# SSD decay factors made during the gate products and carried through DRAM, and a new placement of the scan's first tiles

## The chip, the cores and the metric

One core of one Trainium2 chip runs the whole layer as one program. The metric is the device time of that program in microseconds (us), as the median over runs. Before the change it is 1986.23 us (three runs, 1985.98 to 1989.51).

## The reference, cut to what matters

The layer is a bidirectional hybrid block on 512 positions and 2048 channels in float32: a Mamba-2 SSD branch and a latent attention branch, merged by sigmoid gates. The change touches the diagonal blocks of the SSD scan. For a chunk of 128 positions and one head:

```
da    = dt * a
a_cs  = cumsum(da)                      # along the chunk
lmat  = exp(segsum(da))                 # lower triangle: exp of sums of da between s and l
cb    = einsum("bclgn,bcsgn->bcgls", cc, bc)
y_diag = einsum("bcgls,bgjcls,bcsgjp->bclgjp", cb, lmat, xd)
```

The scan runs forward and, on flipped sequences with its own `dt` and `a`, backward; both results are added. There are 32 heads in 4 groups and 4 chunks. The decay factors `lmat` depend only on `dt` and `a`, which are known long before the scan needs them.

## The kernel before

**Stages.** The program first normalizes `x` and makes `dt` (to about 110 us of the trace), then the three gate products `wz`, `wgs`, `wga` (to about 563 us), then the scan of the four groups, interleaved with projections that fill TensorE (to about 1120 us), then attention, two output projections and the last product. Float32 products are made of three fp32r matmuls: high by high, high by low, low by high.

**How a weight reaches TensorE.** A chunk of 128x1024 weights is loaded by SyncE's DMA queue (L493, tiles `X`, `Y` and `wraw`). ScalarE casts it to its high part `wh` (L457), VectorE subtracts to get the low part `wl` (L458), and TensorE runs 12 matmuls on it (L603 to L605). `wh` and `wl` have three buffers each. The gate products are Strassen products in column pairs: `pair` (from L689) makes seven products P1, P5, P6, P2, P3, P7, P4 of four chunks each, so 28 chunks, and there are three gates with two pairs each. Between products VectorE adds weight chunks (`X` plus `Y` L720, `X` plus `wraw` L724) and results (L650, L655, L678, L736, L757), and GpSimd's queue issues DMAs that add a second block onto a loaded chunk in place (`w_more`, L530) and pre-added weights for later products (L509, L510). Functions hung on `hooks` run after a product by name.

**How the scan makes its factors.** `ssd_group` (from L958) loops over chunks `c` and halves `q` of a group's eight heads. `da_load` broadcasts four heads' rows of `da` from DRAM to 128 partitions, once for each direction (`da0`, `da1`, L1089). `seg_make` runs one cumulative sum with a mask over each (`tensor_tensor_scan`, L1098), adds both (L1101), takes the exponential on ScalarE (L1102, tile `E`), and multiplies `E` into `G` (L1109), the weights of the matmuls `yb` (L1119). There are 32 such factors `E` of 128x512.

**What sets the order.** TensorE's order is written by hand. The other engines' orders come from a list scheduler: it takes operations by priority (program place, moved earlier by `high_priority`) as soon as its own model has their inputs and buffers ready, and the result is fixed in the program. On the chip each engine runs its list in order and waits at whatever is not ready. `keep_in_program_order` pins single instructions. The pool tag `st` (in `gp`) has three tiles of 128x512; before, it serves evictions and is nearly unused in the gate products. Pools are laid over memory of closed pools, and a new tile waits for the old tiles that it covers.

## Time and profile before

| | |
|---|---|
| median of three runs | 1986.23 us |
| the profiled execution, by its own time | 1987.53 us |
| its span in the profile | 1985.8 us |
| TensorE busy | 1933.5 us, 97% |
| VectorE busy | 1476.5 us, 74% |
| ScalarE busy | 1029.3 us, 52% |
| GpSimd busy | 246.3 us, 12% |

All positions below are us from the start of that span. A busy time is the union of an engine's instructions; TensorE's instructions overlap, so its busy share says little about how full it is, and the idle time in front of an instruction, with what ended it, says more. The line numbers are those of the kernel before.

### The profile page before, as it was taken

What the parts mean: (1) busy time and instruction counts of PE and PEld (TensorE: products, weight loads), DVE (VectorE), ACT (ScalarE), POOL (GpSimd) and SP (SyncE); (2) the same over time, 40 slices, a digit from 0 to 9 for tenths busy, and PEclk for the clock granted to TensorE, in tenths of its full rate; (3) what the DMA queues carried; (4) which work ended last, traced back from release to release, by engine and by line L of the source; (5) the groups of instructions that cost most, each with busy time, mean ns of one, the idle gap of its engine ahead of it and who ended that gap; (6) DMA issues with size and microseconds to landing.
All of it is one profiled execution on the core that took longest, in us unless ns stands there. A gap on an engine that the chain in (4) does not pass through costs nothing.

```text
span 1985.8 us, 24464 instructions
## 1 busy us (share of the span) xinstructions
PE 1933.5 (97%) x8834; PEld 1593.3 (80%) x8834; DVE 1476.5 (74%) x2064; ACT 1029.3 (52%) x1527; POOL 246.3 (12%) x309
## 2 busy tenths in 40 slices
PE   7999999999999999999999999999989999999997
PEld 5878888888878878877878878888877778888886
DVE  7876676676759879798785667676776889879467
ACT  6445445444464757747657344444455455444353
POOL 0011001001012020120210101111011111100011
PEclk9999999999999999999999999999999999999999
DMA  5569659569654635655554857787378787847446
GB/s 215 168 198 251 177 159 252 159 166 248 155 174 142 198 122 163 213 182 182 162 165 143 244 149 206 206 223 192 90 219 311 234 271 283 295 140 241 167 87 158
DMA packets 169545, 382.81 MB, mean 193 GB/s; under 512 B 16400, under 2 KB 66256, under 8 KB 169232
## 3 DMA queue, kind: packets, MB, share of 16 engines
q1 hardware_dynamic: 103680, 234.02, 35.2%
q0 software_dynamic: 30656, 103.30, 22.9%
q10 hardware_dynamic: 35088, 43.94, 6.2%
q8 instruction: 69, 1.13, 0.2%
q14 instruction: 52, 0.43, 0.1%
HBM read 329.22 MB, written 98.04 MB: 215 GB/s over the span
## 4 chain that ended last, share of the span: by engine, by line
PE 79%; DVE 9%; DMA 5%; issue 4%; ACT 2%; POOL 1%; SPq 0%; ACTq 0%; DVEq 0%; POOLq 0%
PE P L604 11%; PE P L605 11%; PE P L603 11%; PE xbc L167 4%; PE xbc L168 4%; PE xbc L169 4%; PE za L169 2%; PE za L167 2%; PE za L168 2%; DVE sum L1098 2%; PE qkv L167 1%; PE qkv L169 1%; PE f L1603 1%; PE f L1604 1%; PE qkv L168 1%
## 5 line engine op out<-in xcount | busy, mean ns | idle before, releaser
L457 ACT CAST wh<-X 128x1024 fp32r<-128x1024 f32 x164 | 172.4, 1054 | 203.1 <-PE P L605 154.5
L458 DVE TENSOR_TENSOR wl<-X,wh 128x1024 fp32r<-128x1024 f32 x164 | 199.8, 1222 | 92.2 <-ACT wh L457 91.7
L163 DVE TENSOR_TENSOR wl<-wraw,wh 128x1024 fp32r<-128x1024 f32 (+2 forms) x150 | 176.0, 1174 | 85.9 <-ACT wh L162 80.3
L162 ACT CAST wh<-wraw 128x1024 fp32r<-128x1024 f32 (+2 forms) x150 | 144.7, 967 | 115.6 <-PE xbc L168 34.4
L458 DVE TENSOR_TENSOR wl<-Y,wh 128x1024 fp32r<-128x1024 f32 x88 | 107.5, 1223 | 67.5 <-ACT wh L457 67.5
L167 PE MATMUL xbc<-h_h,wh 128*128 128x512 f32 x384 | 152.8, 398 | 0.0
L457 ACT CAST wh<-Y 128x1024 fp32r<-128x1024 f32 x88 | 92.5, 1054 | 113.6 <-PE P L605 103.7
L169 PE MATMUL xbc<-h_h,wl 128*128 128x512 f32 x384 | 149.8, 390 | 0.0
L168 PE MATMUL xbc<-h_l,wh 128*128 128x512 f32 x384 | 149.6, 390 | 0.0
L603 PE MATMUL P<-wh,h_h 128*128 128x512 f32 x384 | 149.4, 389 | 0.0
L604 PE MATMUL P<-wl,h_h 128*128 128x512 f32 x384 | 149.4, 389 | 0.0
L605 PE MATMUL P<-wh,h_l 128*128 128x512 f32 x384 | 149.4, 389 | 0.0
L457 ACT CAST wh<-wraw 128x1024 fp32r<-128x1024 f32 x68 | 71.7, 1054 | 116.9 <-PE P L605 63.5
L458 DVE TENSOR_TENSOR wl<-wraw,wh 128x1024 fp32r<-128x1024 f32 x68 | 83.1, 1222 | 61.0 <-ACT wh L457 61.0
L604 PE MATMUL P<-wl,S 128*128 128x512 f32 x288 | 112.3, 390 | 0.8 <-DVE wl L458 0.8
L603 PE MATMUL P<-wh,S 128*128 128x512 f32 x288 | 112.1, 389 | 0.5 <-ACT wh L457 0.5
L605 PE MATMUL P<-wh,S 128*128 128x512 f32 x288 | 112.1, 389 | 0.0
L169 PE MATMUL za<-h_h,wl 128*128 128x512 f32 x256 | 100.0, 391 | 1.6 <-DVE wl L163 1.6
L167 PE MATMUL za<-h_h,wh 128*128 128x512 f32 x256 | 101.5, 397 | 0.0
L168 PE MATMUL za<-h_l,wh 128*128 128x512 f32 x256 | 99.7, 389 | 0.0
L169 PEld LDWEIGHTS xbc<-h_h,wl 128*128 128x128 f32 x384 | 72.1, 188 | 15.5
L603 PEld LDWEIGHTS P<-wh,h_h 128*128 128x128 f32 x384 | 72.1, 188 | 15.0
(740 smaller groups left out, 5068.0 us busy)
## 6 DMA issues: line engine op xcount, KB each, us to landing
wraw<-wi SPq DMA_DIRECT2D x102, 512.0 KB, 3.6
T_wps<-wps POOLq DMA_DIRECT2D x32, 512.0 KB, 10.8
da<-da_d SPq DMA_DIRECT2D x64, 256.0 KB, 4.1
T_wpa<-wpa POOLq DMA_DIRECT2D x32, 512.0 KB, 9.2
wraw<-wps SPq DMA_DIRECT2D x24, 512.0 KB, 5.9
wraw<-wo SPq DMA_DIRECT2D x20, 512.0 KB, 3.9
xbc_d<-xbc ACTq DMA_DIRECT2D x24, 256.0 KB, 2.7
wraw<-wun SPq DMA_DIRECT2D x16, 384.0 KB, 4.6
```

Source lines behind the costliest of these rows:

```text
L162: act.copy(h, raw)
L163: dve.tensor_sub(l, raw, h.bitcast(F32))
L167: pe.matmul(out, wh, xh, start=start, stop=False)
L168: pe.matmul(out, wh, xl, start=False, stop=False)
L169: pe.matmul(out, wl, xh, start=False, stop=stop)
L457: i = act.copy(hi_, raw)
L458: dve.tensor_sub(lo_, raw, hi_.bitcast(F32))
L603: pe.matmul(bs[i], xh, wh, start=(j == 0), stop=False)
L604: pe.matmul(bs[i], xh, wl, start=False, stop=False)
L605: pe.matmul(bs[i], xl, wh, start=False, stop=(j == 7))
L1098: dve.tensor_tensor_scan(sums[-1], flat(da), mask, 0.0, ALU.add, ALU.mult)
L1603: pe.matmul(acc, mh, wh, start=(start and k == 0), stop=False)
```

## The change

The 32 factors `E` are no longer made in the scan. A new function `e_make` is hung on the gate products: after P5, P2, P3, P7 and P4 of all six pairs, and after P1 too in the first five. Each call takes a pair of loaded `da` tiles, runs the two masked sums in place on VectorE, adds the second, reversed, into the first on GpSimd (before: VectorE), takes the exponential on ScalarE, stores the result to a DRAM tile `e_d` by ScalarE's DMA queue, and issues the loads of the next pair on SyncE's queue. The pairs live in the three `st` tiles. One load stands ahead of all. In the scan, `seg_make` only takes an `E` that SyncE's queue has fetched (one load of 128x512 for each factor, three buffers instead of two). The masks `scn` are loaded at the start of the gate products, into the place that was a pad of the same size.

The second part gives the scan's later tiles (`r`, `E`, `G`, `cbf`, `cbb`, `yz`, `yo`, `xT`) their places in the pool `sw` first, so that the tiles that are filled first (`BT`, `CT`, the `xs`) lie further on, over the operand sums of the gate products, whose last use is earlier.

Core of the diff:

```diff
+ONCE_MORE = {(0, 0): ("P1",), (0, 1): ("P1",), (1, 0): ("P1",), (1, 1): ("P1",), (2, 0): ("P1",)}
+    e_d = {(g, c, q): scratch(f"e_d{g}{c}{q}") for g in range(GROUPS) for c in range(TT) for q in range(2)}
...
+    scn = wx.tile([P, 2 * SEQ], F32, tag="scn", bufs=1, name="scn")
+    act.dma_start(scn, a["scn"])
+    e_left, e_now = deque(e_d), deque()
+
+    def e_load():
+        if e_left:
+            g, c, q = e_left.popleft()
+            ts = [st(f"da{dd}") for dd in range(2)]
+            for dd, t in enumerate(ts):
+                h0 = dd * NH + g * HPG + q * 4
+                src = da_d[h0:h0 + 4, c * P:(c + 1) * P]
+                nc.sync.dma_start(heads4(t), src.unsqueeze(0).broadcast_to([P, 4, P]))
+            e_now.append((e_d[g, c, q], ts))
...
+    def e_make():
+        if e_now:
+            dst, ts = e_now.popleft()
+            for t, mask in zip(ts, (scn[:, :SEQ], scn[:, SEQ:])):
+                dve.tensor_tensor_scan(t, t, mask, 0.0, ALU.add, ALU.mult)
+            f, b = (heads4(t) for t in ts)
+            pool.tensor_add(f, f, b[:, :, ::-1])
+            act.activation(ts[0], ts[0], AF.Exp)
+            put(dst, ts[0])
+        e_load()
+
+    for g_ in gates:
+        for cp in range(2):
+            for name in ("P5", "P2", "P3", "P7", "P4") + ONCE_MORE.get((gates.index(g_), cp), ()):
+                g_.hooks.setdefault((cp, name), []).insert(0, e_make)
     gates[0].first_columns(0)
+    e_load()
     run(xbc_gen(0, 3, None))
...
+    for tag, n, shape in (("r", 6, [P, SEQ]), ("E", 3, [P, 4, P]), ("G", 2, [P, 4, P]), ("cbf", 2, [P, P]), ("cbb", 2, [P, P]),
+                          ("yz", 2, [P, SEQ]), ("yo", 1, [P, TT, SEQ]), ("xT", 1, [P, TT, SEQ])):
+        for _ in range(n):
+            sw.tile(shape, F32R if tag == "r" else F32, tag=tag, bufs=n, name=f"{tag}_place")
...
-        def da_load(c, q):
+        def e_fetch(c, q):
+            es.append(sw.tile([P, 4, P], F32, tag="E", bufs=3, name="E"))
+            tc.keep_in_program_order(nc.sync.dma_start(flat(es[-1]), e_d[g, c, q]))
...
-            for da, mask in zip(das.popleft(), (scan_f, scan_b)):
-                sums.append(tmp2("sum"))
-                dve.tensor_tensor_scan(sums[-1], flat(da), mask, 0.0, ALU.add, ALU.mult)
-            sf, sb = (t.rearrange("p (h l) -> p h l", h=4) for t in sums)
-            E = sw.tile([P, 4, P], F32, tag="E", bufs=2, name="E")
-            dve.tensor_add(E, sf, sb[:, :, ::-1])
-            act.activation(flat(E), flat(E), AF.Exp)
+            E = es.popleft()
```

TensorE's order is the same in both programs. The other engines' lists differ, and three places show how. The first is VectorE at the end of the first pair of `wz` (P4) and the start of the second (P1, P5). In these rows `wl` is a weight's low part, `u` a result sum, and `X<-X,Y` a weight sum; the numbers are tile numbers, which differ between the programs. Before:

```order
L458 TENSOR_TENSOR wl_1572<-X_1569,wh_1571 128x1024
L458 TENSOR_TENSOR wl_1591<-X_1588,wh_1590 128x1024
L655 TENSOR_TENSOR u_1251<-u_1251,P4_1495 128x512
L655 TENSOR_TENSOR u_1252<-u_1252,P4_1496 128x512
L458 TENSOR_TENSOR wl_1610<-X_1607,wh_1609 128x1024
L458 TENSOR_TENSOR wl_1629<-X_1626,wh_1628 128x1024
L458 TENSOR_TENSOR wl_1656<-X_1569,wh_1655 128x1024
L720 TENSOR_TENSOR X_1569<-X_1569,Y_1653 128x1024
```

In the changed program the same place of VectorE's list reads as follows; `da0` and `da1` are the two tiles of a pair, and L881 is the masked sum.

```order
L881 SCALAR_TENSOR_TENSOR da1_1839<-da1_1839,scn_974 128x512
L657 TENSOR_TENSOR u_1306<-u_1306,P4_1577 128x512
L460 TENSOR_TENSOR wl_1682<-X_1679,wh_1681 128x1024
L657 TENSOR_TENSOR u_1307<-u_1307,P4_1578 128x512
L881 SCALAR_TENSOR_TENSOR da0_2003<-da0_2003,scn_974 128x512
L460 TENSOR_TENSOR wl_1701<-X_1698,wh_1700 128x1024
L460 TENSOR_TENSOR wl_1720<-X_1717,wh_1719 128x1024
L460 TENSOR_TENSOR wl_1756<-X_1660,wh_1755 128x1024
L722 TENSOR_TENSOR X_1660<-X_1660,Y_1753 128x1024
L881 SCALAR_TENSOR_TENSOR da1_2004<-da1_2004,scn_974 128x512
L460 TENSOR_TENSOR wl_1775<-X_1679,wh_1774 128x1024
```

The sums of the ninth and tenth pair now stand between the low parts. The second place is GpSimd's list at the same point of the program (L509 and L510, now L511 and L512, are the pre-added weights; L530, now L532, adds onto a loaded chunk). Before:

```order
L509 DMA T1_wps0_199<-wps 128x1024
L510 DMA T1_wps0_199<-wps 128x1024
L530 DMA X_1569<-wz 128x1024
L530 DMA X_1588<-wz 128x1024
L530 DMA X_1607<-wz 128x1024
L530 DMA X_1626<-wz 128x1024
```

The changed list has the additions of pairs (L883) between and behind these DMAs:

```order
L883 TENSOR_TENSOR da0_1745<-da0_1745,da1_1746 128x512
L532 DMA X_1660<-wz 128x1024
L883 TENSOR_TENSOR da0_1838<-da0_1838,da1_1839 128x512
L532 DMA X_1679<-wz 128x1024
L532 DMA X_1698<-wz 128x1024
L532 DMA X_1717<-wz 128x1024
L883 TENSOR_TENSOR da0_2003<-da0_2003,da1_2004 128x512
L511 DMA T3_wps0_232<-wps 128x1024
L512 DMA T1_wps0_231<-wps 128x1024
L883 TENSOR_TENSOR da0_2090<-da0_2090,da1_2091 128x512
```

So the addition of a pair stands between its own sums and the loads that reuse its tile. The third place is SyncE's DMA queue from the `X` loads of the second pair on. Before:

```order
L493 DMA X_1569<-wz 128x1024
L493 DMA X_1588<-wz 128x1024
L493 DMA X_1607<-wz 128x1024
L493 DMA X_1626<-wz 128x1024
L493 DMA wraw_1864<-wz 128x1024
L493 DMA wraw_2355<-wgs 128x1024
```

In the changed program (L871 loads a `da` tile):

```order
L495 DMA X_1660<-wz 128x1024
L495 DMA X_1679<-wz 128x1024
L871 DMA da0_1838<-da_d_523 128x4x128
L495 DMA X_1698<-wz 128x1024
L871 DMA da1_1839<-da_d_523 128x4x128
L495 DMA X_1717<-wz 128x1024
L871 DMA da0_2003<-da_d_523 128x4x128
L871 DMA da1_2004<-da_d_523 128x4x128
L871 DMA da0_2090<-da_d_523 128x4x128
L871 DMA da1_2091<-da_d_523 128x4x128
```

The loads of `da` stand among the weight loads, and each waits for a tile of `st` to come free. Over the whole program the scheduler has placed the 32 pairs of sums ahead of their hooks: the last pair stands at the 94th of the 168 weight chunks of the gate products, in the second pair of `wgs`, ten pairs to every 28 chunks.

More of the change, by code (lines that the diff above doesn't have):

```diff
@@ L825, in build @@
     cols = part_ = wx
[L826 removed]
+    for tag, n, w in (("X", 4, 1024), ("p1", 2, SEQ), ("p5", 2, SEQ), ("u", 2, SEQ), ("scn", 1, 1024), ("Y", 4, 1024)):
         for _ in range(n):
@@ L867, in build @@
     sp = open_pool("sp", reuse_waits="tile")
-    scn = sp.tile([P, 2 * SEQ], F32, name="scn")
-    act.dma_start(scn, a["scn"])
-    scan_f, scan_b = scn[:, :SEQ], scn[:, SEQ:]
     dsk = sp.tile([P, P], F32, name="dsk")[:, :NH]
```

17 lines of the change are left out of this document (5 added, 12 removed).

## The prediction

> **What bounds the kernel now.** I read the busy times by stage first, then TensorE's own waits, then the groups and DMA landings that price the moved steps. The table of stretches gives the gate products (115 to 560), the scan (560 to 1040) and, from a second question, one column pair of a gate alone:
>
> ```profile
> 115.00:560.00 445.00, 443.78 (x1957) 366.68 (x1956) 305.40 (x295) 211.44 (x236) 53.67 (x66) 1.00 0.70 189
> 560.00:1040.00 480.00, 470.50 (x2240) 388.96 (x2239) 394.52 (x624) 307.25 (x531) 77.15 (x56) 1.00 0.54 172
> ...
> 183.00:259.00 76.00, 76.00 (x337) 62.90 (x337) 51.78 (x51) 35.72 (x41) 9.76 (x12) 1.00 0.72 193
> ```
>
> The columns are the stretch, its length, busy time of TensorE, its weight loads, VectorE, ScalarE and GpSimd, the granted clock, the DMA engines' share and GB/s. In the gates TensorE is full and VectorE has about a third free; in the scan VectorE is busy 394.52 of 480 us (82%) and TensorE idles 9.5 us. A pair's 28 weight chunks take 76 us, 2.72 us each. TensorE's waits in the scan, then in the gates:
>
> ```profile
> PE pb L971 <- ACT dec L345: 2.2, 1, 2.2
> PE yb L1119 <- DVE y L1122: 2.0, 1, 2.0
> PE yb L1119 <- DVE G L1109: 1.7, 1, 1.7
> PE za L169 <- DVE wl L163: 1.6, 1, 1.6
> PE loc L168 <- DVE xw_l L1026: 1.3, 3, 0.7
> PE off L168 <- DVE s_l L1042: 0.7, 1, 0.7
> ...
> PE P L604 <- DVE wl L458: 0.8, 1, 0.8
> PE P L603 <- ACT wh L457: 0.5, 1, 0.5
> ```
>
> So there is little to win: 9.5 us of waits in the scan, 7.3 of them on VectorE, and what a wait does to the clock. TensorE's order in time around the wait for `G`:
>
> ```profile
> 912.01 0.39 PE L169 MATMUL qkv<-h_h,wl 128*128 128x512 f32 x1
> 914.07 1.10 PE L1119 MATMUL yb<-xT,G 128*128 128x64 f32 x8 [1.67 <-DVE G L1109]
> 915.30 0.63 PE L168 MATMUL qkv<-h_l,wh 128*128 128x512 f32 x1
> 915.73 0.63 PE L169 MATMUL qkv<-h_h,wl 128*128 128x512 f32 x1
> 918.72 0.39 PE L167 MATMUL qkv<-h_h,wh 128*128 128x512 f32 x1
> 918.95 0.40 PE L168 MATMUL qkv<-h_l,wh 128*128 128x512 f32 x1
> ```
>
> After 1.67 us of idling, matmuls start 0.43 us apart from 915.30 to 918.72 instead of 0.23: eight at 0.20 more, 1.6 us.
>
> **What the scan gets.** These groups leave VectorE and ScalarE there:
>
> ```profile
> L1098 DVE TENSOR_TENSOR_SCAN sum<-da,scn 128x512 f32<-128x512 f32 x64 | 81.0, 1286 | 0.3 <-DVE wl L163 0.3
> L1101 DVE TENSOR_TENSOR E<-sum 128x512 f32<-128x512 f32 x32 | 21.9, 683 | 0.3
> L1102 ACT ACT_TABLE_LOAD x21 | 26.9, 1283 | 0.4
> L1102 ACT ACTIVATE E<-E 128x512 f32<-128x512 f32 x32 | 20.2, 631 | 25.6 <-DVE E L1101 25.4
> ```
>
> VectorE loses 81.0 + 21.9 = 103 us and falls to 292 of 480 us. I let its 7.3 us of waits go, with one slow stretch of 1.6 us, and half of the 2.2 us on `dec`: about 10 us. The ends are 5 us (the four smaller waits alone, 1.7 + 1.6 + 1.3 + 0.7) and 14 us (9.5 plus three slow stretches). `dec` is where the placement acts:
>
> ```profile
> 565.51 7.24 DMA CT<-xbc_d
> 572.78 0.62 ACT c_h L985
> 573.42 1.28 ACT L342
> ```
>
> The load of `CT` is issued only at 565.51 and its landing holds ScalarE, which makes `dec` last. With `BT` and `CT` over sums that die earlier this load can start before the gates' last product ends, so part of the 2.2 us goes; what is late next is the `dt` chain on ScalarE, hence half.
>
> **What the gates pay.** Ten pairs of sums stand in every 28 chunks. VectorE's own work per pair of columns becomes 51.8 + 20 x 1.286 = 77.5 us against 76: already more than TensorE's time. Over the 86 chunks from the second pair of sums to the last it is 86/28 x 51.8 + 62 x 1.286 = 239 us against 86 x 2.72 = 234. The buffers give a little:
>
> ```profile
> 208.63 1.05 ACT L457 CAST wh<-wraw 128x1024 fp32r<-128x1024 f32 x1 [1.66 <-PE P L605]
> ...
> 209.71 1.22 DVE L458 TENSOR_TENSOR wl<-wraw,wh 128x1024 fp32r<-128x1024 f32 x1 [1.34 <-ACT wh L457]
> ```
>
> A chunk's cast begins when TensorE frees a buffer two chunks ahead of its use (5.4 us), and its low part is done 1.05 + 1.22 + 0.03 = 2.3 us later, so VectorE may be 3 us late, once. That leaves 239 - 234 - 3 = 2 us.
>
> The dearer part is a wait inside VectorE's list. Of the two tiles of a new pair, one reuses the tile that the addition of the pair just before it frees; the other reuses an older one, freed by a store. So the chain from pair to pair is: sums, addition on GpSimd, load on SyncE's queue, next sum. The store and the exponential stand in the longer loop over two pairs. The rows for the two links:
>
> ```profile
> L1051 POOL TENSOR_TENSOR yo<-yo,tmp 128x512 f32<-128x512 f32 x24 | 37.8, 1591 | 77.3 <-DVE tmp L1050 68.6 <-ACT xw_h L1025 8.7
> L1022 POOL TENSOR_TENSOR xw<-xT,wst 128x512 f32<-128x512 f32 x24 | 30.1, 1281 | 56.7 <-ACT xT L982 39.9 <-issue 16.7
> ...
> da<-da_d SPq DMA_DIRECT2D x64, 256.0 KB, 4.1
> ...
> wraw<-wgs SPq DMA_DIRECT2D x7, 512.0 KB, 3.2
> X<-wgs SPq DMA_DIRECT2D x8, 512.0 KB, 5.4
> Y<-wgs SPq DMA_DIRECT2D x8, 512.0 KB, 8.4
> ```
>
> The first two are GpSimd's additions and products in the scan, the third is the very load, in the scan; the last three are loads in the gates (110 to 350). I take 1.59 (the same form, two tensors in place) plus 4.0 for the load, just under its row, plus 0.1 for the handovers: L = 5.7 us. The bounds are 1.28 + 3.2 + 0.1 = 4.6 and 1.59 + 5.4 + 0.1 = 7.1. Against L stands the work that VectorE has in its list between a pair's last sum and the sum that waits for that load. In the rows of the changed order it is `u`, `wl`, `u` from the ninth to the tenth pair, and these cost:
>
> ```profile
> L458 DVE TENSOR_TENSOR wl<-X,wh 128x1024 fp32r<-128x1024 f32 x164 | 199.8, 1222 | 92.2 <-ACT wh L457 91.7
> L720 DVE TENSOR_TENSOR X<-X,Y 128x1024 f32<-128x1024 f32 x44 | 53.7, 1223 | 1.2
> L650 DVE TENSOR_TENSOR p<-p,P 128x512 f32<-128x512 f32 x20 | 13.6, 679 | 0.0
> ```
>
> That is 0.68 + 1.22 + 0.68 = 2.6 us, and VectorE stands still for 5.7 - 2.6 = 3.1. Counted so through the order, the 31 links have 1.2 us of work three times, 2.6 three times, 3.7 nine times, 5.05 six times, 6.2 four times and 7.4 or more six times. The sum of what is missing to 5.7 is 3 x 4.5 + 3 x 3.1 + 9 x 2.0 + 6 x 0.65 = 45 us. Since VectorE's work alone fills the stretch, none of it is made good: the low parts behind the waiting sum come late, and TensorE waits for them. With L = 4.6 the sum is 24 us, with 7.1 it is 78.
>
> The Trainium skill's page "DMA: Bandwidth & Descriptors", section "Anatomy of one DMA", prices a DMA at 2.0 us plus its bytes over 436 GB/s, an estimate of 2.6 us for this load; the wait would be 20 us and the whole sum 12 us above before. The trace's own row for the load is 4.1, so I don't go by it.
>
> What else moves is covered as long as the chain is not longer. ScalarE gains ten exponentials (6.3 us) and about nine table loads (at 1.283) per pair of columns, 35.7 to some 54 of 76 us; if that cover goes, casts come late as the low parts do. The table load stands ahead of the exponential's own wait. Weight loads behind a waiting `da` load on SyncE's queue, and the in-place additions behind a pair's addition on GpSimd's, are put back by the same waits and not by more. Below nothing these cannot go, since they only add work there.
>
> Sum: 2 + 45 in the gates, 10 off in the scan: +37 us. The profiled execution (1987.53, span 1985.8) lies 1.3 us over the median; the median becomes 1986.2 + 37 = 2023 us. The low end is 2 + 24 - 14 = +12, 1998 us. The high end is 2 + 78 - 5 = +75, and 8 more if the five or so longest waits each slow the clock by 1.6 us: 2069 us.
>
> The page "TensorE: Matmul & The Clock Gate", section "Part 1: The HAM clock gate", says that the array falls to half clock after an idle window of about 3.4 us. The 1.67 us above were enough for it here, so by that row the waits of 2.0 and 3.1 us may do it too, and by the page's length only the longest, 4.5 us, would. Since a slowed array is caught up in the next wait for VectorE, I put neither into the middle value.
>
> **Rivals.**
> *The waits are hidden (faster).* The order is safe if the chain is short: at L = 3.2 us the wait is 3 x 2.0 + 3 x 0.6 = 8 us and with the 2 it just eats the scan's 10. For it: loads of `wraw` land in 3.2. Against it: GpSimd's row alone is 1.28 at the least, so the load would have to land in under 1.9. With no wait left the time is 1986 - 10 = 1976 us. 9%.
> *It cancels (same).* At L near 3.4 the time stays within 4 us, 1982 to 1990. 4%.
> *The DMA engines fill up (much slower).* In the scan SyncE's queue moved
>
> ```profile
> q1 hardware_dynamic: 48252, 61.07, 42.2%
> ```
>
> (packets, MB, share of 16 engines) in 465 us (575 to 1040), so 61.07 MB took 196 us of all 16 engines, 0.31 MB a microsecond. Two loads and a store are 0.79 MB, 2.5 us; ten are 25 us per 76, 0.33 on top of 0.72. Then loads land as `Y` does, in 8.4: with L = 7.1 everywhere and 10.1 in the six links beside the `Y` loads the wait is 78 + 18 = 96 us, the time 1986 + 2 + 96 - 10 = 2074 us. Against it: a slower TensorE also asks for fewer bytes. 13%.
> *The scan doesn't get faster (the change doesn't give what it takes).* TensorE was full for 470.5 of 480 us, and its waits could pass to ScalarE, busy 307. Then 1986 + 47 = 2033 us, within the forecast's range. 8%.
>
> **How the numbers follow.** The forecast has 66%, and with the third and fourth rival slower has 66 + 13 + 8 = 87%; same is 4% and faster 9%, where 0.2% (4 us) is about what a measurement of this kernel can tell from no change. The range 1998 to 2069 leaves out the first two rivals and about half of the third.
>
> **What would show it.** In the changed profile VectorE should be busy nearly all the time from about 130 us until the last pair of sums, with idle time in front of the sums (L881) ended by DMAs, some 45 us in all, and TensorE should wait for `wl` by about as much there; the gates should end near 610 instead of 563 us. The loads of `da` should land in about 4 us. In the scan VectorE should be near 290 us busy and TensorE's waits on it gone. I am wrong if the gates end where they did, if the idle time stands in front of casts or weight loads rather than sums, or if landings in the gates are below 2 us.

## The result, and the profile after

| us | before | changed |
|---|---|---|
| median | 1986.23 (5 runs, 1982.91 to 1989.51) | 2121.95 (5 runs, 2118.01 to 2126.72) |
| span of the profiled execution | 1985.8 | 2120.1 |
| first to last product of the gates | 103.1 to 561.8 = 458.7 | 104.3 to 704.7 = 600.4 |
| last product of the gates to the first attention score `s` | 618.4 | 607.0 |
| first `s` to the end | 805.6 | 808.4 |

The changed kernel takes 1.069 times as long, with a 95% interval of 1.067 to 1.072. The difference of the spans, 134.3 us, is 141.7 more in the gates, 11.4 less from there to the first `s`, 2.8 more behind it and 1.2 ahead of the gates. The scan gained about what was forecast. The whole miss lies in the gates.

The table of stretches, for the gates before, the gates after, and 480 us of scan from the gates' end after (the columns are the stretch, its length, busy time of TensorE, its weight loads, VectorE, ScalarE and GpSimd, granted clock, DMA share, GB/s):

```profile
103.10:561.80 458.70, 457.48 (x2017) 378.03 (x2015) 314.35 (x304) 218.20 (x243) 57.02 (x71) 1.00 0.71 192
```

```profile
104.30:704.70 600.40, 501.89 (x2016) 396.76 (x2015) 405.33 (x369) 266.84 (x300) 118.86 (x104) 0.93 0.70 190
...
702.90:1182.90 480.00, 477.40 (x2287) 396.75 (x2286) 313.14 (x554) 263.04 (x488) 73.71 (x56) 1.00 0.48 157
```

Read the first two rows as two losses. TensorE idles 600.4 - 501.9 = 98.5 us where it idled 1.2, and the same matmuls keep it busy 44.4 us longer, because the granted clock falls from 1.00 to 0.93. The DMA share is the same 0.70, over a longer time. In the scan TensorE is busy 477.4 of 480 us, where it was 470.5. TensorE's waits after, in the gates and then in the scan:

```profile
PE P L606 <- DVE wl L460: 95.8, 40, 11.1
PE P L605 <- ACT p L568: 2.1, 1, 2.1
...
PE loc L170 <- DVE xw_l L1063: 1.9, 4, 0.7
PE off L170 <- DVE s_l L1079: 0.7, 1, 0.7
```

The scan's waits for `dec`, `y`, `G` and the weights' low parts are gone, 9.5 us have become 2.6. In the gates TensorE waits for low parts, and the groups say what VectorE, GpSimd and ScalarE wait for ahead of their new work:

```profile
L881 DVE TENSOR_TENSOR_SCAN da<-da,scn 128x512 f32<-128x512 f32 x64 | 82.1, 1284 | 124.7 <-DMA da<-da_d 120.9 <-DMA scn<-scn 3.7
L883 POOL TENSOR_TENSOR da<-da,da 128x512 f32<-128x512 f32 x32 | 61.4, 1918 | 236.1 <-DVE da L881 208.4 <-DMA Y<-wgs 14.7 <-DMA X<-wz 13.0
L884 ACT ACTIVATE da<-da 128x512 f32<-128x512 f32 x32 | 20.2, 631 | 117.3 <-POOL da L883 117.2
```

VectorE stands still for 124.7 us in front of the sums, 120.9 of it for `da` loads; ScalarE stands still for 117.2 us in front of the exponentials, with the casts of weights behind them in its list. Idle time is no loss by itself: it is one where something due stands behind it. The queues' own waits show the same on SyncE, before and after:

```profile
SPq L493 <- DVE wl L458: 344.8, 61, 35.0
```

```profile
SPq L495 <- DVE wl L460: 181.9, 45, 35.0
SPq L871 <- POOL da L883: 101.2, 31, 6.3
SPq L871 <- DMA e_d<-da: 94.4, 20, 11.8
SPq L871 <- DMA da<-da_d: 74.1, 14, 12.8
```

Before, SyncE waited mostly for a weight buffer to come free: it was far ahead. After, it stands 270 us in front of `da` loads (L871) whose tiles are not free, with weight loads behind them. Matching each sum to its load and each load to what freed its tile, the 120.9 us are 66.8 behind loads that had waited for an addition, 42.9 behind loads that had waited for a store, and 11.2 behind loads for which the trace shows neither wait.

### The profile page after: what moved, and what is told of

Its sections match the earlier page's. It is cut to its first block, busy times and chain, and to the rows that moved or that the text cites. A ratio compares the mean times of both kernels' runs of the same rounds, so it can differ in the third digit from the quotient of the medians.

```text
span 2120.1 us, 24720 instructions
## 1 busy us (share of the span) xinstructions
PE 1976.3 (93%) x8834; PEld 1612.2 (76%) x8834; DVE 1474.7 (70%) x2032; ACT 1019.5 (48%) x1518; POOL 304.0 (14%) x341
## 4 chain that ended last, share of the span: by engine, by line
PE 63%; DVE 8%; DMA 7%; issue 3%; ACT 1%; POOL 1%; SPq 0%; DVEq 0%; POOLq 0%; ACTq 0%
PE P L606 7%; PE P L607 7%; PE P L605 6%; PE xbc L169 3%; PE xbc L170 3%; PE xbc L171 3%; DMA da<-da_d 2%; PE za L169 2%; PE za L170 2%; PE za L171 2%; DVE wl L460 2%; PE qkv L169 2%; PE qkv L171 2%; PE qkv L170 2%; DMA wraw<-wps 1%
## 5 line engine op out<-in xcount | busy, mean ns | idle before, releaser
L460 DVE TENSOR_TENSOR wl<-X,wh 128x1024 fp32r<-128x1024 f32 x164 | 209.5, 1285 | 55.7 <-ACT wh L459 55.6
L606 PE MATMUL P<-wl,h_h 128*128 128x512 f32 x384 | 160.5, 418 | 49.4 <-DVE wl L460 49.4
L881 DVE TENSOR_TENSOR_SCAN da<-da,scn 128x512 f32<-128x512 f32 x64 | 82.1, 1284 | 124.7 <-DMA da<-da_d 120.9
L606 PE MATMUL P<-wl,S 128*128 128x512 f32 x288 | 119.2, 414 | 46.5 <-DVE wl L460 46.5
L605 PE MATMUL P<-wh,h_h 128*128 128x512 f32 x384 | 158.0, 411 | 0.0
L607 PE MATMUL P<-wh,h_l 128*128 128x512 f32 x384 | 157.9, 411 | 0.0
L606 PEld LDWEIGHTS P<-wl,h_h 128*128 128x128 f32 x384 | 77.4, 202 | 74.7 <-DVE wl L460 58.3
L459 ACT CAST wh<-wraw 128x1024 fp32r<-128x1024 f32 x68 | 71.4, 1052 | 108.9 <-PE P L607 44.4
L605 PE MATMUL P<-wh,S 128*128 128x512 f32 x288 | 115.9, 402 | 2.6 <-ACT p L568 2.1
L607 PE MATMUL P<-wh,S 128*128 128x512 f32 x288 | 115.9, 402 | 0.0
L606 PEld LDWEIGHTS P<-wl,S 128*128 128x128 f32 x288 | 56.5, 196 | 67.7 <-DVE wl L460 56.3
L169 PE MATMUL za<-h_h,wh 128*128 128x512 f32 x256 | 101.5, 397 | 0.0
```

The source lines that it names most:

```text
L169: pe.matmul(out, wh, xh, start=start, stop=False)
L459: i = act.copy(hi_, raw)
L460: dve.tensor_sub(lo_, raw, hi_.bitcast(F32))
L605: pe.matmul(bs[i], xh, wh, start=(j == 0), stop=False)
L606: pe.matmul(bs[i], xh, wl, start=False, stop=False)
L607: pe.matmul(bs[i], xl, wh, start=False, stop=(j == 7))
```

## The experiments

Two theories stood at first. **A**: the pairs stand too close, and each waits for the one before it. **B**: the work does not fit (sums, additions, bytes). Later ones were **C** (the `da` loads hold up SyncE's queue), **D** (the DMA engines are full half the time), **E** (ScalarE waits in its list for additions, or the work itself costs the time) and **W** (the loss is waiting in the order of lists and queues). All kernels start from the changed one unless said otherwise. Their times are medians, and ratios are to the kernel before. "Gates" is the time from the first to the last product of the gates, 458.7 us before the change.

### The second part alone

The kernel before, with only the loop of places added ahead of the scan's pool:

```diff
+    for tag, n, shape in (("r", 6, [P, SEQ]), ("E", 2, [P, 4, P]), ("G", 2, [P, 4, P]), ("cbf", 2, [P, P]), ("cbb", 2, [P, P]),
+                          ("yz", 2, [P, SEQ]), ("yo", 1, [P, TT, SEQ]), ("xT", 1, [P, TT, SEQ])):
+        for _ in range(n):
+            sw.tile(shape, F32R if tag == "r" else F32, tag=tag, bufs=n, name=f"{tag}_place")
```

> The kernel before with the loop of places alone at the head of the scan's pool (buffers for r, E, G, cbf, cbb, yz, yo, xT laid first), the sums left in the scan. The prediction gave the placement half of the 2.2 us that TensorE waits on dec: 1985 us, a change within 0.2%. If the placement is worth the whole of what the scan gained (11.4 us from the gates' last product to the first s), 1975 us, and no wait pb<-dec. If it puts a new wait in, over 1990 us.

1983.26 us, ratio 0.9991 (0.9979 to 1.0003): no difference that can be told. The wait that it should shorten is still there, whole:

```profile
PE pb L976 <- ACT dec L345: 2.2, 1, 2.2
```

So the placement alone does not do what the prediction gave it, and its mechanism is not there either: the load of `CT` was to be issued before the gates' last product ends, but it is issued 3.7 us after that product's start before the change, 3.6 in `place_only` and 3.7 in the changed kernel. In the changed kernel the wait for `dec` is gone only together with the other part; which piece of that does it is open.

### The scan and the stores alone

`store_only` leaves out the `da` loads, the sums, the additions and the exponentials, and stores the mask's tile in their place, so that the scan reads factors that are not `E`. The part in `e_make`:

```diff
-            for t, mask in zip(ts, (scn[:, :SEQ], scn[:, SEQ:])):
-                dve.tensor_tensor_scan(t, t, mask, 0.0, ALU.add, ALU.mult)
-            f, b = (heads4(t) for t in ts)
-            pool.tensor_add(f, f, b[:, :, ::-1])
-            act.activation(ts[0], ts[0], AF.Exp)
-            put(dst, ts[0])
+            tc.keep_in_program_order(act.dma_start(dst, scn[:, :SEQ]))
```

> The changed kernel with the making of E left out: no da loads, no sums, no additions, no exponentials in the gates; the 32 stores are issued from ScalarE's list, in program order, straight from the mask's tile, so that the scan reads factors that are not E. It gives the gain of the scan alone with the stores' price. All theories that put the loss into the chain in the gates: gates 459 to 464 us, scan as in the changed kernel (607 against 618 us to the first s), the rest +3: total 1976 to 1983 us. If the loss hangs on the stores or on the scan's fetches, over 2000 us.

1977.16 us, ratio 0.996 (0.994 to 0.997), the gates 458.1 us. The scan's gain is real, the 32 stores cost nothing, and 1977 is the floor against which the making of `E` is priced below.

### Spacing and tiles

`sums_pinned` holds the sums in program order; `five_tiles` gives the even pairs two tiles of their own, in the mask's place, so that its sums read another constant as the mask and their values are left out; `five_pinned` does both.

```diff
-                dve.tensor_tensor_scan(t, t, mask, 0.0, ALU.add, ALU.mult)
+                tc.keep_in_program_order(dve.tensor_tensor_scan(t, t, mask, 0.0, ALU.add, ALU.mult))
```

```diff
-            ts = [st(f"da{dd}") for dd in range(2)]
+            ts = [wx.tile([P, SEQ], F32, tag="dd", bufs=2, name=f"da{dd}") if len(e_left) % 2 else st(f"da{dd}") for dd in range(2)]
...
-            for t, mask in zip(ts, (scn[:, :SEQ], scn[:, SEQ:])):
+            for t, mask in zip(ts, (cst[:, :SEQ], cst[:, P:P + SEQ])):
```

> The changed kernel with the 64 sums held in program order on VectorE, so that the 32 pairs stand spread over all 168 chunks (10 to 12 sums in 28 chunks, pairs mostly 4 to 9 chunks apart and twice per 28 next to each other) instead of 20 sums in 28 chunks. Same work, same three tiles, same bytes. Theory A (the waits of a pair on the pair before it, because the pairs stand closer than the chain through GpSimd, store and load is long): VectorE's idle time in front of the sums falls from 124.7 us to 20 to 40, and the gates from 600 to about 465 to 485 us; total 1985 to 2005 us. Rival B (the work itself does not fit: sums on VectorE, additions on GpSimd, 25 MB more for the DMA engines): the gates stay over 540 us and the total over 2060 us.

> The changed kernel with two more tiles for the pairs (even pairs in two tiles of their own, odd pairs in the shared three), in the place of the mask; the sums read other constants as the mask, so the values of the sums are left out of the computation and the work is the same. The order now packs the 32 pairs into 70 chunks (26 sums in 28 chunks). Theory A: a pair no longer waits for the addition of the one before it but for the one two before; the idle time in front of the sums falls to under 60 us, and what is left is VectorE's own excess, 51.8 + 26 x 1.286 = 85 against 76 us per 28 chunks, 23 us in all: total 2005 to 2040 us. Rival B (the work does not fit): denser is worse or the same, 2100 to 2140 us. Rival C (it is the da loads standing in SyncE's queue ahead of the weight loads): between the two, with TensorE's waits on wh and wl behind late landings of X and wraw.

> Sums held in program order as in sums_pinned, and two more tiles for the pairs as in five_tiles (the sums read other constants as the mask; the work is the same, the values of the sums are left out). A load of da no longer waits for the pair just before. In sums_pinned SyncE's queue stood 188 us for stores of E, 135 us for additions and only 49 us for the low parts that free the weights' buffers (345 us before the change): Theory C (weight loads stand in SyncE's queue behind da loads that wait for their tiles, and come late): that waiting goes, gates 462 to 485 us, total 1980 to 2005 us. Theory B (the work or the bytes do not fit): nothing that is counted as work changes, total 2060 to 2085 us.

| | us | idle before the sums | gates |
|---|---|---|---|
| changed kernel | 2121.95 | 124.7 | 600.4 |
| sums_pinned | 2077.02 | 58.0 | 559.6 |
| five_tiles | 2136.40 | 101.5 | 618.4 |
| five_pinned | 2056.83 | 15.5 | 532.6 |

Theory A is a part and not the whole. With the pairs spread over all 168 chunks 45 us come back, and 101 us of gates stay. Two more tiles alone make it slower; the order then packs the pairs closer still, into 70 weight chunks instead of 93. With both, the idle time before the sums is nearly gone, and 74 us of gates stay: the sums are not where the rest is lost. The longest wait left in `sums_pinned` shows something else (VectorE's list at 310, then the table of stretches over the time from that load's issue to its landing):

```profile
310.03 2.34 DVE L881 TENSOR_TENSOR_SCAN da<-da,scn 128x512 f32<-128x512 f32 x2 [10.20 <-DMA da<-da_d]
```

```profile
295.50:309.90 14.40, 8.58 (x38) 6.76 (x36) 4.33 (x4) 7.67 (x10) 3.85 (x3) 0.96 0.99 224
```

The load took 14.4 us, with the DMA engines full (0.99).

### Sums left out; the loads on another queue

`no_sums` leaves out both sums (and pins the additions instead); `pool_loads` and `act_loads` are `sums_pinned` with `nc.sync` of the `da` loads replaced by `pool` or `act`.

```diff
-                nc.sync.dma_start(heads4(t), src.unsqueeze(0).broadcast_to([P, 4, P]))
+                pool.dma_start(heads4(t), src.unsqueeze(0).broadcast_to([P, 4, P]))
```

> The loads, the additions on GpSimd (held in program order, so that the pairs stand spread as in sums_pinned), the exponentials and the stores as in the changed kernel; the 64 sums on VectorE, 82 us of work, are left out of the computation. Theory C: the da loads still wait in SyncE's queue for the additions and stores, so most of the loss stays: total 2030 to 2080 us. If VectorE's work is the cause: gates 460 to 470 us, total 1976 to 1990 us.

> As sums_pinned, with the 64 da loads issued by GpSimd instead of SyncE. SyncE's order of weight loads becomes the one of before, word for word; same three tiles, same waits of a load on the addition and the store, same bytes. Theory C: the X, Y and wraw loads come early again; what waits behind a da load is now GpSimd's own list, where the in-place additions from DRAM onto X and Y stand, so part of the loss stays there: total 1990 to 2050 us, with SyncE waiting mostly for wl again. Theory B: 2065 to 2090 us.

> As sums_pinned, with the 64 da loads issued from ScalarE's list instead of SyncE's queue. Theory C: SyncE's queue is free, but a load that waits 6 to 8 us for a store now holds ScalarE, which has two chunks (5.4 us) of lead on TensorE: total 1995 to 2060 us, with TensorE's waits moved from wl to wh. Theory B: 2065 to 2090 us with the same waits as in sums_pinned.

Without the sums the kernel takes 2081.48 us, no less than `sums_pinned`: taking VectorE's 82 us of sums out gains nothing while the rest of the chain stays. What TensorE and ScalarE wait for there:

```profile
PE P L605 <- ACT wh L459: 51.0, 17, 7.3
PE P L606 <- DVE wl L460: 17.1, 26, 0.9
...
ACT da L882 <- POOL da L881: 130.5, 21, 9.2
```

The exponential waits in ScalarE's list for an addition, which waits for a load, and the casts behind it come late. The chain has moved from VectorE's list to ScalarE's. So VectorE's work alone, as theory B had it, does not make the loss; what it costs when the rest does not wait, this run cannot say.

`pool_loads` takes 2053.93 us, 23 less than `sums_pinned`. SyncE's order of weight loads is then that of before, and its wait for low parts is that of before too (344.8 us); the waiting loads now hold GpSimd:

```profile
SPq L495 <- DVE wl L460: 345.3, 62, 40.7
...
POOL da L871 <- DMA e_d<-da: 89.0, 14, 12.9
```

So theory C holds for these 23 us. `act_loads` takes 2083.04 us, about as `sums_pinned`. TensorE's waits did not move to `wh`, as had been expected (68.2 us for `wl`), but ScalarE stands longer ahead of the exponentials, 108.2 us against 78.2. Here a load that has to wait costs as much in ScalarE's list as in SyncE's queue.

### Loads without compute, compute without loads

`loads_only` keeps the `da` loads and the stores and leaves out sums, additions and exponentials; `compute_only` leaves out the loads, and its sums read `h_l`, which lies in SBUF. The edit of `compute_only`:

```diff
-                nc.sync.dma_start(heads4(t), src.unsqueeze(0).broadcast_to([P, 4, P]))
...
-                dve.tensor_tensor_scan(t, t, mask, 0.0, ALU.add, ALU.mult)
+                tc.keep_in_program_order(dve.tensor_tensor_scan(t, h_l[:, 0, :].bitcast(F32), mask, 0.0, ALU.add, ALU.mult))
```

> The 64 da loads (held in program order on SyncE) and the 32 stores (from the loaded tile) stay; sums, additions and exponentials are left out of the computation. Theory D: the loads alone hold the weights back: gates over 510 us, total over 2025 us. Theory E: 1976 to 1990 us, since nothing is left that an engine other than the queues could wait for.

> As sums_pinned, with the 64 da loads left out: the sums read low parts of h that lie in SBUF, so their values are left out of the computation; sums, additions, exponentials with their table loads and the stores of E stay, at the same places and in the same three tiles. Theory D (the loads: 16.8 MB that land in the half of each 76 us in which the DMA engines were full before the change, share 0.93 to 1.05 from 227 to 265 us against 0.01 to 0.28 from 196 to 215, and that hold SyncE's queue meanwhile): gates 459 to 475 us, total 1978 to 1995 us. Theory E (in-order waits of ScalarE for GpSimd's additions and the work itself): over 2020 us.

`loads_only` takes 2013.13 us and `compute_only` 2005.81, 36 and 29 over the floor. Neither theory had this right: each half costs something, and 36 + 29 = 65 is less than the 100 of `sums_pinned`, where both are. In `compute_only` ScalarE still stands in front of exponentials:

```profile
ACT da L880 <- POOL da L879: 54.1, 22, 6.5
```

Issuing each of those one step later (`compute_late`) was tried next to it:

```diff
     def e_make():
+        if e_sums:
+            dst, t = e_sums.popleft()
+            tc.keep_in_program_order(act.activation(t, t, AF.Exp))
+            tc.keep_in_program_order(act.dma_start(dst, t))
...
-            act.activation(ts[0], ts[0], AF.Exp)
-            put(dst, ts[0])
+            e_sums.append((dst, ts[0]))
```

> compute_only (2006 us, no loads) with each exponential and its store issued one step later, ahead of the next pair's sums, so that ScalarE never waits for an addition that has just been asked for (54 us of such waits in compute_only). Theory W: the 29 us over store_only (1977) go: 1977 to 1988 us. If instead VectorE's 82 us of sums or ScalarE's table loads cost them: 1998 to 2010 us.

1998.07 us, in a wide spread (1989.78 to 2008.41, 7 runs), at the lower edge of the second expectation. ScalarE's waits for additions are gone, and some 8 of the 29 us with them, with an uncertainty as large; the rest goes with the work itself or with its other waits.

### When the DMA engines are free

In the table of stretches of the kernel before, two stretches of one pair of columns and the same two one pair later:

```profile
195.70:214.70 19.00, 19.00 (x85) 15.73 (x84) 14.99 (x14) 8.42 (x10) 0.00 (x0) 1.00 0.19 47
233.70:252.70 19.00, 19.00 (x86) 15.73 (x85) 12.07 (x13) 9.44 (x12) 0.00 (x0) 1.00 1.00 321
271.70:290.70 19.00, 19.00 (x85) 15.74 (x84) 15.00 (x14) 8.42 (x10) 0.00 (x0) 1.00 0.16 43
309.70:328.70 19.00, 19.00 (x85) 15.73 (x85) 12.07 (x13) 9.44 (x12) 0.00 (x0) 1.00 1.01 313
```

The share of 0.72 that the prediction quotes is a mean over stretches of 0.16 to 0.19, of 1.00 and of values in between. So the pairs were put where the engines are free, by counting the chunks:

```diff
+    for i_ in range(7):
+        for k_ in (-1, 1, 3, 5, 7, 9):
+            ticks.setdefault(28 * i_ + k_, []).append(e_make)
...
             h, l = w_split(raw)
+            tick()
```

> All work stays (sums with other constants as the mask, five tiles, sums held in program order, loads on SyncE, as in five_pinned, 2057 us), but the pairs are made from places two chunks apart in the eleven chunks of every 28 in which the DMA engines were nearly idle before the change, so that SyncE's order is again four Y and four X loads in a row, and the da loads stand behind them among the loads of wraw. Theory D: the X and Y loads land as before, TensorE's waits go almost wholly: total 1978 to 2000 us. Theory E or B (the work): packed work in 11 chunks, 12 x 1.286 = 15.4 us of sums beside some 22 us of other work of VectorE in 30 us, is worse than spread, over 2057 us.

> The changed kernel with the real mask and its three tiles, nothing left out; only the places of the pairs are those of five_timed. Pairs stand two chunks (5.4 us) apart, the chain from pair to pair (addition 2.1, load 3.1 to 4 when the DMA engines are free, handover) takes some 6 to 7 us and the store's loop some 10 over two pairs: VectorE waits 1 to 4 us in each of 5 links of 28 chunks, part of it covered by its own spare time. Theory D: 1985 to 2030 us, better than sums_pinned (2077) though the pairs stand closer together. Theory A (only the spacing matters): worse than sums_pinned, over 2077 us.

2063.51 and 2096.77 us: both miss. With five tiles this is no better than the spread version (2057; the intervals of the ratios overlap), with three it is worse by 20 us (2077), as theory A had it. The same matmuls that ran in the two free stretches before, from 195.70 and from 271.70, run here in these:

```profile
211.60:240.90 29.30, 23.03 (x85) 17.19 (x84) 24.75 (x20) 10.48 (x13) 6.33 (x3) 0.88 0.54 138
299.10:335.40 36.30, 21.52 (x85) 16.63 (x84) 25.59 (x20) 10.79 (x13) 6.43 (x3) 0.86 0.44 121
```

What took 19.0 us takes 29.3 and 36.3, and the DMA engines are not full in it (0.54 and 0.44). VectorE's work there is 24.8 and 25.6 us, where it was 15.0: it does not fit a stretch of 19 us, whatever the loads do. That placing alone is enough falls too.

### Nothing waits for what was just started

`five_even` makes one pair every five chunks (13.6 us). A step first issues the next pair's loads into tiles freed a step ago (three for the forward sums, two for the backward ones), then the exponential and store of the pair before, whose addition is long done, then this pair's sums and addition. Like `five_tiles` it reads another constant as the mask. `even_real` does so with the real masks, each sum made as four of 128 columns, and leaves nothing out; `even_pool` issues its loads from GpSimd; `even_small` is `even_pool` with a quarter of the bytes in each load, and its sums read `h_l` instead, so their values are left out.

```diff
+    def e_store():
+        dst, t = e_sums.popleft()
+        tc.keep_in_program_order(act.activation(t, t, AF.Exp))
+        tc.keep_in_program_order(act.dma_start(dst, t))
+
     def e_make():
+        e_load()
+        if e_sums:
+            e_store()
...
+    for k_ in range(0, 168, 5):
+        ticks[k_] = [e_make]
```

```diff
-                src = da_d[h0:h0 + 4, c * P:(c + 1) * P]
-                tc.keep_in_program_order(pool.dma_start(heads4(t), src.unsqueeze(0).broadcast_to([P, 4, P])))
+                src = da_d[h0:h0 + 1, c * P:(c + 1) * P]
+                tc.keep_in_program_order(pool.dma_start(t[:, :P], src.broadcast_to([P, P])))
```

> All the work of the changed kernel (other constants as the mask, so the sums' values are left out), five tiles, but nothing in an engine's list waits for what was started just before: one pair every 5 chunks (13.6 us); the load of a pair is issued one step ahead into tiles that have long been free, its exponential and store one step after its addition. Theory W (the loss is in-order waiting, in SyncE's queue, in front of sums and in front of exponentials): gates 462 to 485 us, total 1976 to 2000 us, idle time in front of the sums under 15 us. Theory D (16.8 + 8.4 MB more for DMA engines that are full half the time): X, Y and wraw land late whatever the order, total over 2030 us. Both: 2000 to 2030 us.

> The same order as five_even with the real masks, nothing left out: the forward mask is read from a constant that is resident anyway, the backward one is cut to one head's 128 columns, so each sum is made as four of 128 columns (8 instead of 2 instructions per pair, estimated from 1.2 us per 512 as 0.35 to 0.45 us each, so 10 to 35 us more on VectorE in all, which has some 130 us free in the gates). Theory W: 1978 to 2005 us, the first correct version within 1% of the kernel before, or under it. Theory D: over 2030 us.

> even_real with the da loads issued by GpSimd, so that SyncE's order is that of before. If SyncE's queue is still what holds the weights in even_real, it is faster by what SyncE waits there; if the DMA engines are, the same within 5 us. GpSimd's own issue of a load costs 0.6 to 0.9 us by the rows of its other DMAs, 64 x 0.9 = 58 us on an engine that is busy 12% here, ahead of in-place additions onto X and Y: up to 15 us slower if those come late.

> even_pool (2007 us, nothing in a list waits for what was started just before) with each da load cut to one head, 64 instead of 256 KB, 12.6 MB less in all; the sums read low parts of h in its place, so their values are left out; instructions, places, tiles and waits are unchanged. Theory D for the remainder (DMA engines full half the time, so X, Y and wraw land later): most of the 30 us over store_only goes, total 1978 to 1992 us, X from SyncE's queue lands in 5 to 6 us as before instead of 7 to 10. If the remainder is the work (107 us of sums on VectorE, 32 exponentials with two table loads each on ScalarE) or the issue of loads on GpSimd: 2000 to 2010 us.

| | us | ratio (95%) | gates |
|---|---|---|---|
| five_even | 2019.39 | 1.018 (1.016 to 1.019) | 505.3 |
| even_real | 2027.93 | 1.023 (1.021 to 1.025) | 517.2 |
| even_pool | 2006.59 | 1.011 (1.010 to 1.013) | 492.0 |
| even_small | 1990.73 | 1.003 (1.002 to 1.005) | 475.8 |

The order in time alone takes `five_pinned` from 2057 to 2019 us, with all its work and bytes. SyncE still stands for stores there:

```profile
SPq L880 <- DMA e_d<-da: 183.2, 27, 18.8
```

A step of 13.6 us is not always enough for an exponential, a store and what stands ahead of them. Freeing SyncE's queue gives 21 us more (`even_real` to `even_pool`), close to the 23 of `pool_loads`. With 12.6 MB less to move, another 16 us go (`even_small`), so theory D holds for these. VectorE's waits for `da` loads fell only from 4.1 to 1.9 us, so that the small loads themselves land sooner explains little of it. The gates of `even_pool` and `even_small`:

```profile
103.10:595.10 492.00, 469.96 (x2017) 376.43 (x2015) 402.35 (x559) 282.17 (x312) 182.28 (x165) 1.00 0.82 231
```

```profile
104.60:580.40 475.80, 464.49 (x2017) 377.62 (x2016) 400.97 (x558) 282.77 (x312) 169.84 (x165) 1.00 0.79 213
```

The `X` loads of `wgs` on SyncE's queue land in 7.0 us in `even_pool` and in 6.3 in `even_small`, against 5.4 before, so not in the 5 to 6 us that had been expected. This landing is no measure of the loss: it is 4.8 us in the changed kernel, the slowest of the four, and 8.5 in `compute_only`, which has no `da` loads. Of the 14 us that are left over the floor the runs show no cause. They are less than the 21 that `compute_late` keeps without any loads, so the work in the lists may be all of them; how it would divide among VectorE, ScalarE and GpSimd was not separated.

### Half of the pairs

The kernel before, with 16 pairs made as in `even_pool`, one every ten chunks, and 16 left in the scan:

```diff
+    e_d = {(g, c, 0): scratch(f"e_d{g}{c}") for g in range(GROUPS) for c in range(TT)}
...
+    for k_ in range(0, 168, 10):
+        ticks[k_] = [e_make]
...
+            made = das.popleft()
+            if len(made) == 1:
+                E = made[0]
+            else:
...
```

> The kernel before with half of the factors (16 pairs, one every 10 chunks) made in the gates in the manner of even_pool and the other half left in the scan; nothing left out. If the price in the gates is in proportion, 16 us against 5 to 6 us won in the scan: 1992 to 2000 us. If the price comes from crowding (full DMA engines, lists without slack) and falls faster than the number of pairs, 3 to 6 us against 5 to 6: 1980 to 1986 us, no difference that can be told. Under 1979 us it would beat both kernels.

1982.38 us, ratio 0.9984 (0.9973 to 0.9996), the gates 464.9 us. Half the pairs cost 6 us of gates where all of them cost 33: the price falls much faster than their number, as crowding would have it. The interval just leaves out 1, but 0.16% is under the 0.2% that the prediction took as telling, so this is at most a trace of a gain; no version here that makes every factor `E` beats the kernel before by more than 0.16%.

## Why the prediction was wrong: right in sign, a hundred microseconds short

**The scan** came out as forecast in size: 10 us less forecast, 11.4 measured. VectorE fell from 394.5 to 313.1 us of 480, not to 292, in part since the 480 us now hold some 10 us of later work. Half of the `dec` wait was given to the placement; all of it went, but `place_only` shows that the placement alone takes none, and the load of `CT` did not start earlier. That this small term of the sum still fits is luck.

**VectorE's own work**, 2 us, did not bind the stretch. VectorE should have been busy nearly all the time until the last pair; from 115 to 500 us it was busy 257.4 of 385 us. It stood still behind `da` loads instead.

**The step that failed is the wait inside VectorE's list**, "L = 5.7 us", and with it the "45 us" that were added up from it, and the clock's 0 beside it. The gates took 141.7 us more, against 47 forecast: 97.3 are idle time of TensorE and 44.4 slower matmuls. For the wait the mechanism was the one named, and TensorE's 95.8 us for `wl` behind 124.7 in front of the sums are its mark. Three things made it larger.

- *The chain was too short.* The addition took 2.12 us at the median, not 1.59, and the loads 4.7, not 4.0. By the prediction's own table L = 6.9 would have given about 73 us. None of the 64 loads landed in the 2.6 us that the prediction estimated by the Trainium skill's page "DMA: Bandwidth & Descriptors", section "Anatomy of one DMA"; that section is about DMAs that GpSimd issues, and these loads stand on SyncE's queue. And a chain was priced with one landing, where the trace has 3.1 to 15.7: the sixth pair's load landed 13.9 us after its issue, and its sum waited 11.77. VectorE's list there, and the table of stretches from that load's issue to its landing, with the DMA engines at 0.97:

```profile
166.46 1.22 DVE L881 TENSOR_TENSOR_SCAN da<-da,scn 128x512 f32<-128x512 f32 x1 [2.62 <-DMA da<-da_d]
167.60 1.20 DVE L460 TENSOR_TENSOR wl<-Y,wh 128x1024 fp32r<-128x1024 f32 x1
180.57 1.23 DVE L881 TENSOR_TENSOR_SCAN da<-da,scn 128x512 f32<-128x512 f32 x1 [11.77 <-DMA da<-da_d]
```

```profile
166.60:180.60 14.00, 3.65 (x15) 2.36 (x13) 2.23 (x3) 3.20 (x4) 2.98 (x2) 0.87 0.97 220
```

- *The loop through the store binds too.* "The store and the exponential stand in the longer loop over two pairs" dropped it; 42.9 of the 120.9 us stand behind loads that had waited for a store. So the loop over two pairs was often longer than two pairs take.
- *The lists in between were taken as covered.* "Weight loads behind a waiting `da` load on SyncE's queue ... are put back by the same waits and not by more" is wrong by some 21 to 23 us, by the two pairs of runs with the loads on SyncE and on GpSimd, though at other spacings than the changed kernel's. The exponentials, covered likewise, stood 117.2 us in ScalarE's list; what this alone cost was not separated.

**The clock was put at 0**, "since a slowed array is caught up in the next wait for VectorE". It was not: the same matmuls took 44.4 us more, and in the gates the granted clock was 0.93. TensorE around the longest wait:

```profile
171.50 0.39 PE L605 MATMUL P<-wh,S 128*128 128x512 f32 x1
182.97 0.79 PE L606 MATMUL P<-wl,S 128*128 128x512 f32 x1 [11.08 <-DVE wl L460]
183.56 0.63 PE L607 MATMUL P<-wh,S 128*128 128x512 f32 x1
183.98 0.63 PE L605 MATMUL P<-wh,S 128*128 128x512 f32 x1
184.41 0.63 PE L606 MATMUL P<-wl,S 128*128 128x512 f32 x1
```

From 183.56 the matmuls start 0.43 us apart instead of 0.23. Counted so in the trace, all 14 waits of 2.65 us and more, and two of the four from 2.04 to 2.18, are followed by 7 to 13 matmuls that start 0.38 us or more apart, 145 in all and 31 us over 0.23 each; the nine from 1.17 to 1.75 are followed by none. So a long wait is paid for twice, with some 2 us behind it; the other 13 of the 44.4 us are open. The Trainium skill's page "TensorE: Matmul & The Clock Gate", section "Part 1: The HAM clock gate", puts the idle window at about 3.4 us. Here 2.08 was enough once, and 1.67 in the prediction's row; in `even_pool` one wait of 2.56 was followed by no slow matmul, so the runs give no sharp length.

**The rival of the full DMA engines** (2074 us) was dismissed by half because the share was read as a mean, 0.72. It holds stretches of 0.19 and of 1.00, and a load that meets a full stretch lands late, as the rows at 166.60 show. It was part of the cause: 12.6 MB less were worth 16 us in `even_pool`, where the waits had been taken out.

From 2122 to 1977 us the runs give one path: 45 us for spacing, 20 for two tiles, 37 for asking a step ahead (`five_pinned` to `five_even`), 13 for SyncE's queue less the cost of the shorter sums (`five_even` to `even_pool`), 16 for the bytes, and 14 that are left without a shown cause. The parts depend on each other (65 apart, 100 together), so another order of steps would give other prices.

## What to carry to other kernels

Work moved into an engine's free time needs lead before it needs room: ask for every step of the chain what it waits for, where in its list that wait stands, and what is due behind it, on the queues too. A dependent chain through a DMA has to be priced with its slow landings, and a mean DMA share has to be cut into stretches first. If all stages of a chain are issued in one place, move each a whole step apart before moving anything else.

## What the runs showed of the hardware that was not expected

**An addition on GpSimd and an instruction of VectorE with two inputs in SBUF hold each other up, a sum by scan too.** GpSimd's addition took 1.26 to 1.30 us in 8 of 32 cases and 2.03 to 2.19 in 24. Three cases, in GpSimd's list and (after each) VectorE's, where x2 is two sums in one row:

```profile
157.92 1.30 POOL L883 TENSOR_TENSOR da<-da,da 128x512 f32<-128x512 f32 x1 [10.33 <-DVE da L881]
156.57 3.73 DVE L881 TENSOR_TENSOR_SCAN da<-da,scn 128x512 f32<-128x512 f32 x2
...
406.07 2.06 POOL L883 TENSOR_TENSOR da<-da,da 128x512 f32<-128x512 f32 x1 [12.54 <-DVE da L881]
404.73 2.33 DVE L881 TENSOR_TENSOR_SCAN da<-da,scn 128x512 f32<-128x512 f32 x2
406.98 2.24 DVE L460 TENSOR_TENSOR wl<-Y,wh 128x1024 fp32r<-128x1024 f32 x1
...
363.90 2.11 POOL L883 TENSOR_TENSOR da<-da,da 128x512 f32<-128x512 f32 x1 [12.56 <-DVE da L881]
363.68 1.20 DVE L460 TENSOR_TENSOR wl<-X,wh 128x1024 fp32r<-128x1024 f32 x1
364.91 2.18 DVE L722 TENSOR_TENSOR X<-X,Y 128x1024 f32<-128x1024 f32 x1
```

At 404.73 two sums take 2.33 us, and the addition, which starts after the second one has begun, takes 2.06. At 157.92 the addition starts just ahead of the second sum and takes 1.30, and the two sums take 3.73. In all 24 slow cases VectorE had started a sum, a low part or a weight sum 0.2 to 0.3 us before the addition; in the 8 fast ones nothing of the kind was running. Such an instruction that VectorE starts during an addition is held in its turn: 2.24 and 2.18 us in the rows, where 1.20 is usual. This is what made the addition's 2.12 us in the chain. The Trainium skill's page "SBUF — State Buffer", section "Who interferes with whom", says that a VectorE instruction with two inputs in SBUF contends with a GpSimd instruction that reads SBUF, and that the order of issue decides who is held; the trace agrees, for the scan as for the subtraction.

**A sum's price is not quite by the element:** 128 columns took 0.40 us and 512 took 1.21, so making 64 sums of four short ones each took 14 us more of VectorE's busy time in all (`even_real`, then `five_even`):

```profile
L899 DVE TENSOR_TENSOR_SCAN da<-da,cst 128x128 f32<-128x128 f32 x128 | 45.4, 407 | 10.2 <-DMA da<-da_d 10.2
L899 DVE TENSOR_TENSOR_SCAN da<-da,scn 128x128 f32<-128x128 f32 x128 | 44.6, 402 | 0.0
```

```profile
L895 DVE TENSOR_TENSOR_SCAN da<-da,cst 128x512 f32<-128x512 f32 x64 | 76.0, 1212 | 7.4 <-DMA da<-da_d 7.4
```

**The same DMA share is not the same rate.** In the kernel before, the stretch from 233.70 to 252.70 moved 321 GB/s at a share of 1.00. The one from 189.30 moved 241 with the engines as full:

```profile
189.30:195.70 6.40, 6.40 (x30) 5.31 (x29) 5.38 (x5) 3.85 (x5) 0.00 (x0) 1.00 1.03 241
```

In the second all packets (1.54 MB, 103.0% of the share) are of the queue q0, on which GpSimd's DMAs run, those that add onto chunks and make the pre-added weights. Why they move fewer bytes in the same time is open.
